# Low-rank products on the un-normed input, inverses in 16-token blocks joined by products, and a new order of the recurrence's front

## The chip, the cores and the metric

The kernel runs on one core of one Trainium2 chip. The metric is the device time of one execution in microseconds (us), as a median of runs. The engines named below are TensorE (PE in the profile; its weight loads are PEld), VectorE (DVE), ScalarE (ACT), GpSimd (POOL) and SyncE (SP, which here only issues transfers). Each engine takes its own instructions in order, and semaphores hold it until the data of another are there.

## The reference, cut to what matters

Two transformer blocks on 256 tokens with 1024 features, the first with 16 meta tokens ahead of them, so T = 272. The first block is: FFN, RWKV7 time mix, FFN, FFN, sparse attention, FFN. Everything is float32. The change lies in the time mix, which works on the normed input `h`:

```python
def rwkv7_time_mix(h, mix, w_r, w_k, w_v, w_o, w0, w1, w2, a0, a1, a2, g1, g2, k_k, k_a, r_k, ...):
    xx = jnp.pad(h, ((0, 0), (1, 0), (0, 0)))[:, :-1] - h          # the token before, minus this one
    xr, xw, xk, xv, xa, xg = h[None] + xx[None] * mix[:, None, None, :]
    r = xr @ w_r;  k = xk @ w_k;  v = xv @ w_v
    w_log = -softplus(-(w0 + jnp.tanh(xw @ w1) @ w2)) - 0.5         # w1: 1024 x 64
    a = sigmoid(a0 + (xa @ a1) @ a2)                                # a1: 1024 x 64
    g = sigmoid(xg @ g1) @ g2                                       # g1: 1024 x 160
    kk = k * k_k, normed per head of 64 (norm at least 1e-12)
    k = k * (1.0 + (a - 1.0) * k_a)
    decay = exp(-exp(w_log))
    # per head, state S of 64 x 64, for each token:
    #   S = S * decay + (S @ -kk) (kk * a)^T + v k^T ;  y = S @ r
    ...
    return ((yn + bonus) * g) @ w_o
```

## The kernel before, in words

Activations lie transposed, 128 features on the partitions, eight tiles (KT) of T = 272 tokens. A product of float32 numbers is three products of rounded halves: `mm3` (L260) multiplies hi by hi (L261), lo by hi (L262) and hi by lo (L263). Activations are split into such halves by ACT (`xh`) and VectorE (`xl`, L440), weights by ACT (`wh`, L173) and VectorE (`wl`, L182). Weights come in units of 128 x 1024, by transfers on SP's queue into a ring; `run` and `ahead` load and split some units ahead. A projection of one 128-wide output tile (k0 to k7, v0 to v7, r0 to r7) is one unit of 8 x 3 products of 272 columns.

The time mix (`rwkv`) does not scan token by token. It works in chunks of 64 tokens. Its front is:

- The sums of squares of the first FFN's output (`sumsq`, a hook of the out-projection) go through two products with a matrix of ones (L306, L307) to `rstd`. `first_mix` then makes per tile the normed input `hn` (L499), the difference `xx` (L501, in the buffer kbx) and the mixes: x2 for k (L489, split into xh and xl), x1 and x4 for the low-rank w1 and a1 (also L489, unsplit, xm). A generator `mg` makes x5 for g1 (L463, unsplit).
- `first` does the units k0 to k2 with the 32 low-rank records of w1 and a1 between them (L594, plain f32 products of 272 columns). `l1_unit` does the same for g1 later (L614). The second factors follow (`l2w`, `l2a`, L639).
- Per k unit, `ev_k` squares on ACT (L562) and copies to kf; `ev_kb` sums the squares over a head by a product (L569) and takes the floor (L570, VectorE) into `rn`.
- `decay_a` scans the log decays (L654), `decay_b` takes their exponentials (L663 into AR, L664 in place, `pinv`), `units` the inverse norms (L681, L682) and kk (L684), `keys`, `removal` and `over` multiply the scaled keys (L691 to L717). AR and KB are then the two operands of the products within a chunk, `aab` (L738, L741), evacuated into the tile `tf`/`Dg` (L743).
- `inverses` inverts the unit triangular blocks of 32 tokens, 128 of them side by side, on VectorE: `start` transposes (L874), `rows` eliminates row by row (L868 multiplies, L871 adds, in two halves; the last rows by L885), `end` transposes back (L891, L892). The 16 meta tokens have a small one, `meta` (tile am). Chunks join 32-blocks by doubling products (L1122, L1130).

What order all this has is written by hand in `ORDER`: `play` walks it, takes the names in `UNITS` as weight units and the others as calls between them. The Tile framework's scheduler then sets each engine's queue from that. `early` has slots (tag S), `rk` holds AR, kbx and the rest.

## Time and profile before

| what | us |
|---|---|
| median of 3 runs | 1543.95 (1542.97 to 1545.03) |
| profiled execution, its own time | 1543.19 |
| profiled execution, its span | 1541.3 |
| TensorE busy | 1478.7 (96%) |
| VectorE busy | 1001.5 (65%) |
| ACT busy | 742.6 (48%) |
| mean granted TensorE clock | 0.988 |

The profile is of one execution. Its times count from the start of its span. A busy share is an average over stages with different limits, so the stage is read on its own: which engine is busy in it throughout, and what the others wait for. The granted clock is that of TensorE, where 1.00 is 2.4 GHz and 0.5 is 1.2 GHz. The time mix's front is the stretch from 214.55 us, where the last product of the first FFN ends, to 372 us.

### The profile page before, as it was taken

The page shows a single profiled execution, that of the slowest core. Times are in us where ns is not written, and L with a number is a line of the kernel's source. Part 1 is how long each engine was busy: PE and PEld are TensorE (multiplying, and loading weights), DVE is VectorE, ACT ScalarE, POOL GpSimd, SP SyncE. Part 2 cuts the span into 40 slices and gives each one's busy share as a digit, 9 for nine tenths or more (in the row PEclk, how much of TensorE's full clock was granted, in tenths as well). Part 3 has the DMA queues.
Part 4 walks back from the last instruction along what each step waited for, and adds up shares of the span by engine and source line. Part 5 has one row for each costly group of instructions (what it writes and reads, how often), then busy time and mean ns, then how long its engine had stood idle before and what let it go on. Part 6 is the DMA issues. An engine that isn't in the chain of part 4 may idle for free.

```text
span 1541.3 us, 30953 instructions
## 1 busy us (share of the span) xinstructions
PE 1478.7 (96%) x12612; PEld 1391.7 (90%) x12612; DVE 1001.5 (65%) x1887; ACT 742.6 (48%) x1284; POOL 261.5 (17%) x298
## 2 busy tenths in 40 slices
PE   7999989697999999999999998999999999999999
...
GB/s 227 211 171 167 175 132 123 87 97 69 43 2 178 177 174 164 174 198 169 175 174 164 182 120 59 23 198 192 190 177 185 186 142 96 87 223 190 187 195 99
...
## 3 DMA queue, kind: packets, MB, share of 16 engines
...
HBM read 226.52 MB, written 2.10 MB: 148 GB/s over the span
## 4 chain that ended last, share of the span: by engine, by line
PE 81%; DVE 12%; ACT 3%; issue 2%; DMA 2%; POOL 1%; SPq 0%; DVEq 0%; POOLq 0%; ACTq 0%
PE mm L261 22%; PE mm L263 22%; PE mm L262 22%; DVE wl L182 2%; PE mm L1896 1%; PE mm L1170 1%; PE mm L1169 1%; DMA wf<-ffn_in 1%; PE mm L1171 1%; PE mm L1898 1%; PE mm L1873 1%; PE mm L994 1%; PE mm L1840 1%; PE mm L802 1%; ACT L L1852 1%
## 5 line engine op out<-in xcount | busy, mean ns | idle before, releaser
L173 ACT ACTIVATE wh<-wf 128x1024 fp32r<-128x1024 f32 (+2 forms) x410 | 418.0, 1021 | 543.2 <-issue 277.9
L182 DVE TENSOR_TENSOR wl<-wf,wh 128x1024 fp32r<-128x1024 f32 (+2 forms) x402 | 479.1, 1193 | 144.8 <-PE mm L263 99.6
L261 PE MATMUL mm<-xh,wh 128*128 128x272 f32 (+2 forms) x1888 | 542.4, 289 | 13.4 <-ACT wh L173 8.3
L263 PE MATMUL mm<-xh,wl 128*128 128x272 f32 (+2 forms) x1888 | 541.2, 288 | 3.3 <-DVE wl L182 3.3
L262 PE MATMUL mm<-xl,wh 128*128 128x272 f32 (+2 forms) x1888 | 541.5, 288 | 2.9 <-DVE xl L440 2.5
L261 PEld LDWEIGHTS mm<-xh,wh 128*128 128x128 f32 (+1 forms) x1888 | 356.0, 189 | 18.9 <-ACT wh L173 9.2
L262 PEld LDWEIGHTS mm<-xl,wh 128*128 128x128 f32 (+1 forms) x1888 | 356.2, 189 | 6.1 <-DVE xl L440 3.2
L263 PEld LDWEIGHTS mm<-xh,wl 128*128 128x128 f32 (+1 forms) x1888 | 356.6, 189 | 4.8 <-DVE wl L182 4.5
L261 PE MATMUL mm<-hh,wh 128*128 128x272 f32 (+1 forms) x704 | 201.9, 287 | 0.0
L263 PE MATMUL mm<-hh,wl 128*128 128x272 f32 (+1 forms) x704 | 201.8, 287 | 0.0
L262 PE MATMUL mm<-hl,wh 128*128 128x272 f32 (+1 forms) x704 | 201.8, 287 | 0.0
L352 POOL TENSOR_TENSOR s<-s,rstd 128x272 f32<-128x272 f32 (+1 forms) x88 | 74.2, 845 | 443.9 <-ACT s L351 443.9
L261 PEld LDWEIGHTS mm<-hh,wh 128*128 128x128 f32 x704 | 132.7, 188 | 0.0
L263 PEld LDWEIGHTS mm<-hh,wl 128*128 128x128 f32 x704 | 132.6, 188 | 0.0
L262 PEld LDWEIGHTS mm<-hl,wh 128*128 128x128 f32 x704 | 132.5, 188 | 0.0
L360 DVE TENSOR_TENSOR u<-mm,s 128x272 f32<-128x272 f32 (+1 forms) x88 | 38.4, 437 | 124.8 <-PE mm L263 107.9
L182 POOL TENSOR_TENSOR wl<-wf,wh 128x1024 fp32r<-128x1024 f32 (+3 forms) x44 | 85.4, 1944 | 114.4 <-PE mm L263 38.6
L298 POOL TENSOR_TENSOR acc<-acc,sq 128x272 f32<-128x272 f32 (+1 forms) x48 | 41.5, 864 | 255.4 <-ACT sq L296 247.0
L350 DVE TENSOR_TENSOR t<-mm,rstd 128x272 f32<-128x272 f32 (+1 forms) x88 | 38.2, 436 | 70.7 <-PE mm L263 70.6
L262 PE MATMUL mm<-hid,wh 128*128 128x256 f32 x256 | 72.1, 282 | 0.0
L261 PE MATMUL mm<-hid,wh 128*128 128x256 f32 x256 | 72.1, 282 | 0.0
L263 PE MATMUL mm<-hid,wl 128*128 128x256 f32 x256 | 72.1, 281 | 0.0
...
## 6 DMA issues: line engine op xcount, KB each, us to landing
...
```

The costliest lines, as they stand in the source:

```text
L173: self.A.activation(u.wh, u.wf[:u.p, :u.n], AF.Copy)
L182: (self.V if u.lo == "V" else self.G).tensor_tensor(u.wl, u.wf[:u.p, :u.n], u.wh.bitcast(F32), op=ALU.subtract)
L261: self.mm(out, wh, xh, start=start, stop=False)
L262: self.mm(out, wh, xl, start=False, stop=False)
L263: self.mm(out, wl, xh, start=False, stop=stop)
L298: self.G.tensor_tensor(self.acc[:, :n], self.acc[:, :n], self.sq[:, :n], op=ALU.add)
L350: V.tensor_tensor(t[:, :n], st.pop(("g", m))[:, :n], r, op=ALU.mult)
L352: G.tensor_tensor(s[:, :n], s[:, :n], r, op=ALU.mult)
L360: V.tensor_tensor(u[:, :n], st.pop(("u", m))[:, :n], st.pop(("s", m))[:, :n], op=ALU.mult)
L802: mm(p[:, :T], wf[:w, s], R["lo"][1 + z][:w], start=z == 0, stop=z == 1)
L994: mm(ps[h][:, j * w:(j + 1) * w], flat(src(c, m)[OWN[h]]), R["AR"][OWN[h], m, j0:j0 + n, tok(c)], start=True, stop=True)
L1169: self.mm(out, xh, wh, start=start, stop=False)
```

## The change

Four edits come together.

1. `first_factors`, between gate/up and the out-projection of the first FFN, loads the first low-rank factors and makes w·mix and w·(1 − mix) from them, split into halves. The out-projection's hook splits its output with the gain but without the norm. `low_rank` then does 5 sums of 8 x 3 products on that un-normed input. `ev_l1` multiplies the sums by rstd (each token's own for one factor, shifted by a token for the other) and adds them. L594, L614 and the mixes x1, x4 and x5 are gone.
2. The split mix of k lies in the room of AR (tag "AR"). The floor of the squares is a Relu with a bias on ACT.
3. `inverses` inverts blocks of 16 instead of 32 tokens, both blocks of a 32-block in one operation, 15 rows of two operations; `turned`, `joined` and `added` then join the two by 128, 128 and 64 small products.
4. A new `ORDER` of the front, up to r2; from there it is the old one.

```diff
@@ ORDER, its front
-ORDER = ("mg evk2 evk0 mg mg k3 evk1 l2w evkb2 k4 evkb1 evk3 mg evkb3 decay_a mv mv mv evkb0 l2a k5 k6 evk4 mg "
...
+ORDER = ("lwa k0 lg1 l2w k1 evk0 l2a evk1 evkb0 k2 lg2 tri evk2 evkb1 decay_a k3 mv evk3 evkb2 k4 mv mv evkb3 evk4 "
...
@@ swiglu
+        if between:
+            between()
         self.out_proj(wout, KFF, lambda: st["h"], 0.5, t0, n, hook)
@@ first_factors (new), per factor of 128 columns
+                for s, i in mixes:
+                    o = VEC["mix"] + 8 * i
+                    V.tensor_tensor(b[:, :, s], w[:, :, s], self.vec[:, o:o + KT, None].to_broadcast([128, KT, s.stop - s.start]),
+                                    op=ALU.mult)
+                V.tensor_tensor(a, w, b, op=ALU.subtract)
...
+                    for x in (a, b):
+                        t = slot("l1", F32R, 2 * KT * n)
+                        o = t.rearrange("p (j k c) -> p j k c", j=2, c=n)
+                        A.activation(o[:, 0], x, AF.Copy)
+                        V.tensor_tensor(o[:, 1], x, o[:, 0].bitcast(F32), op=ALU.subtract)
...
+        prepare(0, 128, ((slice(0, 64), 1), (slice(64, 128), 4)))
+        prepare(128, 128, ((slice(0, 128), 5),))
+        prepare(256, 32, ((slice(0, 32), 5),))
@@ first_mix
-            hi, lo = R["x", 2] = [self.xs.tile([128, KT, T], F32R, tag=n, name=n) for n in ("xh", "xl")]
...
+            x2 = R["pool"].tile([128, 2, KT, T], F32R, tag="AR", name="xk")
+            hi, lo = R["x", 2] = x2[:, 0], x2[:, 1]
...
-                for i in (1, 4):
-                    mix(R["x", i][:, k, :T], i, k)
@@ enter
             self.rms(T)
+            low_rank()
             first_mix()
@@ new
+        def low_rank():
+            ps = R["l"] = [self.psum() for _ in range(5)]
+            for k in range(KT):
+                for i, p in enumerate(ps):
+                    w, s = self.l1[i // 2], slice(128 * k, 128 * k + 128) if i < 4 else slice(64 * k, 64 * k + 128)
+                    w = w[i % 2] if i < 4 else w
+                    self.mm3(p[:, :T], w[0][:, s], w[1][:, s], self.xh[:, k, :T], self.xl[:, k, :T], k == 0, k == KT - 1)
+
+        def ev_l1(j):
...
+                V.tensor_tensor(f, p[:n, :T], self.rstd[:n], op=ALU.mult)
+                V.tensor_tensor(y[:, 1:], q[:, :T - 1], r[:, :T - 1], op=ALU.mult)
+                V.tensor_tensor(f[:, 1:], f[:, 1:], y[:, 1:], op=ALU.add)
+                if j == 0:
+                    A.activation(f[:64], f[:64], AF.Tanh)
+                else:
+                    A.activation(f, f, AF.Tanh, scale=0.5)
+                    V.tensor_scalar(f, f, 0.5, 0.5, op0=ALU.mult, op1=ALU.add)
@@ ev_kb
-                V.tensor_scalar(R["rn"][:, m], ss[:, :T], 1e-24, None, op0=ALU.max)
+                A.activation(R["rn"][:, m], ss[:, :T], AF.Relu, bias=self.eps[:, 4:5])
@@ decay_b
+            AR = R["AR"] = R["pool"].tile([128, NP, 2, T], F32, tag="AR", name="AR")
@@ inverses
         def rows(s0, s1):
...
             for s in range(s0, s1):
...
+                m, w = n - 1 - s, s + 1
+                u = self.tmp("u")[:, :2 * m * w].rearrange("p (b i j) -> p b i j", b=2, j=w)
+                below = both(t, w, 0, (B, m), (1, w))
+                V.tensor_tensor(u, both(a, s, w, (1, m), (0, w)), both(t, s, 0, (0, m), (1, w)), op=ALU.mult)
+                V.tensor_tensor(below, below, u, op=ALU.add)
+        def turned():
...
+            V.transpose(Dg[:, :n], tf[:, :, :n].rearrange("p s t -> p t s"))
+            V.transpose(Dt, tf)
+            p = R["p16"] = self.psum()
+            for c in range(32):
+                for r in quads:
+                    mm(p[r, c * n:c * n + n], Dg[r, :, c], Dg[r, :n, c], start=True, stop=True)
+        def joined():
+            V.transpose(Dg[:, n:], tf[:, :, n:].rearrange("p s t -> p t s"))
+            self.A.activation(tf[:, :, :n], byblk(R.pop("p16")), AF.Copy)
+            G.memset(tf[:, :, n:], 0.0)
+            p, o = R["p16"] = self.psum(), self.psum()
+            for c in range(32):
+                for r in quads:
+                    mm(p[r, c * n:c * n + n], tf[r, c], Dt[r, n:, c], start=True, stop=True)
+                for r in quads[::2]:
+                    mm(o[r, c * n:c * n + n], Dt[r, :, c], tf[r, c, :n], start=True, stop=True)
+        def added():
...
+            V.tensor_tensor(x, byblk(p), x, op=ALU.add)
+            for r in quads[::2]:
+                x = Dg[r, :n].rearrange("p t c -> p c t")
+                V.scalar_tensor_tensor(x, byblk(o)[r], self.eps[r, 2:3], x, op0=ALU.mult, op1=ALU.add)
-        cuts = (0, 5, 10, 15, 20, 25, 31)
-        return [start, meta] + [lambda a=a, b=b: rows(a, b) for a, b in zip(cuts[:-1], cuts[1:])] + [end]
+        cuts = (0, 5, 10, 15)
+        return [start, meta] + [lambda a=a, b=b: rows(a, b) for a, b in zip(cuts[:-1], cuts[1:])] + [turned, joined, added, end]
@@ the program
-        c.swiglu(*ffn(0, 0), *full, lambda k: c.sumsq(k, c.h[:, k]), [c.positions(first), c.bias_rows(first)])
+        c.swiglu(*ffn(0, 0), *full, split("norm", 8, *full), [c.positions(first), c.bias_rows(first)], c.first_factors)
```

Line numbers of the changed kernel are 2 higher than before's through most of the file's first part (L261 becomes L263). Three places of the order, engine by engine:

TensorE behind the last product of the first FFN, before: the two products for the norm (on acc and sq) stand next to each other, and the first k product and the low-rank ones (L594, xm by the weight in wf) follow.

```order
L263 MATMUL mm<-hh,wl 128x272
L306 MATMUL mm<-acc,mats 128x272
L307 MATMUL mm<-sq,mats 128x272
L261 MATMUL mm<-xh,wh 128x272
L594 MATMUL mm<-xm,wf 64x272
```

And after, at the same place, to the product on sq (L309); the low-rank weights are the tiles named l_:

```order
L265 MATMUL mm<-hh,wl 128x272
L308 MATMUL mm<-acc,mats 128x272
L263 MATMUL mm<-xh,l_1768 128x272
L264 MATMUL mm<-xl,l_1768 128x272
L265 MATMUL mm<-xh,l_1768 128x272
...
L263 MATMUL mm<-xh,l_1796 128x272
L264 MATMUL mm<-xl,l_1796 128x272
L265 MATMUL mm<-xh,l_1796 128x272
L263 MATMUL mm<-xh,l_1768 128x272
L309 MATMUL mm<-sq,mats 128x272
```

31 of the 120 low-rank products now stand between the product on acc and the one on sq.

ACT around the exponentials of the decay, before: the exponential into AR (L663) comes while k units are still to be squared and copied (L562, L239).

```order
L301 ACT_TABLE_LOAD
L681 ACTIVATE kbx<-kbx 128x1088
L663 ACTIVATE AR<-pinv 128x8x272
L173 ACTIVATE wh<-wf 128x1024
L466 ACTIVATE xmh<-t 128x272 x2
L682 ACTIVATE kbx<-kbx 128x1088
L173 ACTIVATE wh<-wf 128x1024
L562 ACTIVATE s<-mm,vec 128x272
L239 ACTIVATE kf<-mm 128x272
```

And after (L627 is the floor of the squares as a Relu, L665 the exponential into AR, L503 and L508 the mixes of r):

```order
L618 ACTIVATE s<-mm,vec 128x272
L241 ACTIVATE kf<-mm 128x272
L503 ACTIVATE s<-hn,vec 128x272 x2
L627 ACTIVATE kbx<-mm,eps 128x272
L503 ACTIVATE s<-hn,vec 128x272
L627 ACTIVATE kbx<-mm,eps 128x272
L303 ACT_TABLE_LOAD
L665 ACTIVATE AR<-pinv 128x8x272
L683 ACTIVATE kbx<-kbx,eps 128x1088
```

The exponential moved behind the last square, copy and floor of the k units.

TensorE between v7, r0 and r1, before: copies of the keys and values (L970, L982) and the meta products (L1008) follow r0.

```order
L263 MATMUL mm<-xh,wl 128x272
L970 MATMUL mm<-mats,kbx 16x128 x16
L982 MATMUL mm<-mats,vf 16x128 x8
L1008 MATMUL mm<-AR,kbx 16x16 x32
L261 MATMUL mm<-xh,wh 128x272
```

And after, the join's products of `joined` (L913, L915) follow the same copies, 32 pairs of rows like the two shown; those of `turned` (L903, 128 of them) stand ahead of r0:

```order
L265 MATMUL mm<-xh,wl 128x272
L1006 MATMUL mm<-mats,kbx 16x128 x16
L1018 MATMUL mm<-mats,vf 16x128 x8
L913 MATMUL mm<-af,tf 32x16 x4
L915 MATMUL mm<-tf,af 32x16 x2
```

L1008 (now L1044) moved behind r1, and the joins came in between.

## Rows read from the trace of the kernel before

**Rows 1.** The page, TensorE's busy tenths in 40 equal slices of the span.
```profile
PE   7999989697999999999999998999999999999999
```
**Rows 2.** Stretches: length, busy PE, PEld, DVE, ACT, POOL (count), clock, DMA, GB/s.
```profile
219.15:241.65 22.50, 18.79 (x91) 11.89 (x92) 22.50 (x57) 5.14 (x11) 3.25 (x5) 0.85 0.00 1
241.65:269.91 28.26, 27.43 (x173) 24.09 (x173) 22.00 (x37) 24.25 (x46) 0.37 (x2) 1.00 0.54 168
269.91:302.32 32.41, 20.76 (x368) 19.61 (x370) 30.32 (x66) 21.79 (x39) 1.20 (x2) 0.90 0.33 102
302.32:359.07 56.75, 47.13 (x624) 37.60 (x617) 55.30 (x210) 20.31 (x35) 9.16 (x15) 0.95 0.30 94
359.07:371.98 12.91, 11.36 (x171) 9.75 (x172) 4.14 (x11) 6.33 (x12) 4.18 (x4) 0.55 0.00 1
371.98:457.00 85.02, 82.02 (x1342) 67.53 (x1341) 53.77 (x123) 33.94 (x78) 10.10 (x12) 1.00 0.11 33
```
**Rows 3.** Waits of TensorE, 214.55 to 372 us: total us, times, longest.
```profile
PE mm L738 <- DVE AR L717: 8.8, 2, 7.9
PE mm L1122 <- DVE tf L891: 6.2, 1, 6.2
PE mm L261 <- ACT xh L504: 5.1, 1, 5.1
PE mm L741 <- issue: 3.1, 2, 2.1
...
PE mm L1130 <- ACT H L239: 1.5, 2, 1.1
```
**Rows 4.** A stretch of the first FFN, columns as above.
```profile
140.00:150.00 10.00, 10.00 (x82) 10.00 (x81) 5.92 (x9) 4.83 (x8) 1.86 (x2) 1.00 0.59 185
```
**Rows 5.** Timeline at the norm: start, length, engine, line, what, count, [idle before].
```profile
215.89 0.72 PE L307 MATMUL mm<-sq,mats 128*128 128x272 f32 x2 [0.88 <-ACT sq L296]
...
218.67 0.44 DVE L287 SCALAR_TENSOR_TENSOR rstd<-u,rstd 128x272 f32<-128x272 f32 x1
```
**Rows 6.** Groups of VectorE, 214.55 to 302.32 us: count, busy us, mean ns.
```profile
L489 DVE SCALAR_TENSOR_TENSOR xm<-kbx,vec,hn 128x272 f32<-128x272 f32 x16 | 7.2, 489 | 0.0
...
L570 DVE TENSOR_SCALAR kbx<-mm 128x272 f32<-128x272 f32 x8 | 3.2, 430 | 0.0
```
**Rows 7.** Timeline of ACT at the decay's exponential.
```profile
264.64 2.03 ACT L663 ACTIVATE AR<-pinv 128x2176 f32<-128x2176 f32 x1 [0.72 <-DVE pinv L654]
```
**Rows 8.** Timeline: first aab product, AR's end, inverse's transpose, first doubling product.
```profile
285.84 0.24 PE L738 MATMUL mm<-AR,kbx 64*32 64x32 f32 x5 [0.95 <-DVE AR L717]
...
300.99 1.40 DVE L717 TENSOR_TENSOR AR<-AR 128x252 f32<-128x252 f32 x4
...
310.69 2.08 DVE L874 STREAM_TRANSPOSE af<-tf 128x1024 f32<-128x1024 f32 x1
...
359.07 1.10 PE L1122 MATMUL mm<-tf,Tt 32*32 32x32 f32 x32 [6.21 <-DVE tf L891]
```
**Rows 9.** Groups of VectorE, 302.32 to 359.07 us.
```profile
L871 DVE TENSOR_TENSOR tf<-tf,u 128x110 f32<-128x110 f32 (+32 forms) x54 | 11.4, 243 | 0.1
L868 DVE TENSOR_TENSOR u<-af,tf 128x110 f32<-128x110 f32 (+32 forms) x54 | 11.4, 248 | 0.0
L182 DVE TENSOR_TENSOR wl<-wf,wh 128x1024 fp32r<-128x1024 f32 x8 | 9.7, 1209 | 0.0
L871 DVE TENSOR_TENSOR am<-am 128x15 f32<-128x15 f32 (+7 forms) x15 | 2.9, 194 | 0.1
...
L628 DVE TENSOR_SCALAR lora<-lora 128x272 f32<-128x272 f32 (+1 forms) x2 | 1.5, 771 | 0.0
```
**Rows 10.** Timeline of TensorE behind r0.
```profile
330.91 1.93 PE L970 MATMUL mm<-mats,kbx 128*16 128x128 f32 x32
...
334.52 0.69 PE L1008 MATMUL mm<-AR,kbx 64*16 64x16 f32 x64
```
**Rows 11.** The stretch of the first four aab.
```profile
285.84:290.04 4.20, 2.09 (x182) 1.98 (x184) 4.20 (x11) 1.96 (x4) 0.00 (x0) 1.00 0.45 141
```

188 lines of the change are left out of this document (78 added, 110 removed), and 10 rows, old and new, of the table ORDER.

## The prediction

> **What bounds the kernel now.** The page comes first. TensorE is busy nearly everywhere; its thin place is slices 6 to 10 of 40, some 193 to 385 us, with 6 and 7 tenths in the 8th and 10th [rows 1]. That is the front of the RWKV mixer, and every edit lies in it or just ahead of it. Split by stage [rows 2], the front reads: from the norm to 241.65 us VectorE is busy for all of 22.50 us; to the end of the k projections (269.91) TensorE is, for 27.43 of 28.26; then VectorE again, for 30.32 of 32.41 and 55.30 of 56.75, with TensorE idle for 11.7 and 9.6 us of the two and its clock at 0.90 and 0.95; then 12.91 us at a clock of 0.55; from 372 to 457 TensorE is the bound again. The waits say on what TensorE waits there: the decayed keys (L738 on AR, the longest 7.9 us), the inverse (L1122 on the transposed tf, 6.2 us), and the first mix after the norm (L261 on xh, 5.1 us) [rows 3]. So the front is a chain of VectorE work with TensorE filling it, and a saving counts where it moves the end of the last doubling product and the r products behind it (372 us in the trace). I replayed the new order with the durations of the trace, each engine taking its instructions in its own order; the results are below.
>
> The sum is made against the profiled run's own 1543.19 us. The median of the runs, 1543.95, lies 0.8 us above it. A change under 0.2% (3.1 us) can't be told from none in this kernel's measurement.
>
> **Weights made ahead (first_factors).** Some ten VectorE operations and six copies, about 11 and 5 us, stand between gate/up and the out-projection of the first FFN. There VectorE is busy for 5.92 of 10 us and TensorE for all of it, 82 products of 272 columns in 10 us, 0.122 us each [rows 4]. TensorE's cover hides them: 0, at most 2 us if a weight split comes late. The splits of the input in the out-projection's hook lie under its products as the squares did. They are 16 operations, and the last ones have the time that the final products leave.
>
> **The norm, 2.9 us later.** Before, the product with the squares starts at 215.89, and rstd is done 2.54 us after its end, at 219.15 [rows 5]. After, 31 low-rank products stand ahead of it on TensorE: 31 x 0.122 = 3.8 us from 214.9, so it starts at 218.8 and rstd is done at 218.8 + 0.72 + 2.54 = 222.05. In return TensorE isn't idle until 221.69; it does 120 products (14.6 us) up to 230.6, for most of which it had no other work.
>
> **The k projections, 6.3 us shorter.** VectorE sets the pace up to 241.65 and loses 16 xm mixes for the low-rank inputs (7.2 us), 8 of the same kind for the gate (3.6) and 8 floors of the squares (L570, 3.2), which ACT takes [rows 6]: 14.0 us. It gains nine operations of 272 columns at L570's 0.43 and two of the kind of L628 at 0.77 [rows 9], 5.4 us, where the norm is put on the sums. Net 8.6 us. TensorE loses the f32 products of L594 here and of L614 later. In the replay 6.3 of the 8.6 us arrive: TensorE now waits for the tanh of the decay (2.9 us), for free banks (1.3) and for one square (1.4), places where it didn't stand still before. The last k product ends at 222.05 + (269.91 - 219.15 - 6.3) = 266.5, 3.4 us earlier.
>
> **Decays and keys, where the gain is eaten.** The split mix of the k input now lies in the room of AR, so the decay's exponential can't start before the last k product. Before, it started at 264.64, 5.3 us ahead of that product's end, between the k units' own ACT work [rows 7]. After, ACT still has the squares and floors of the last k units and a table load to do, so it starts about 4 us after that end. From there ACT does two large exponentials and four half ones, and VectorE the products of L686, the keys and the removals, with the mixes of r and weight splits between; the replay has the first aab product 28.4 us after the last k product, at 294.9, and AR complete at 300.4. Before, the first came at 285.84, but the second half of them waited for AR, done 302.3 [rows 8]. So TensorE idles from 277 to 295 after v0 to v2, and then has aab, v3 and v4 together. af is transposed at 313, against 312.77 before: the 3.4 us are gone. The nearest short price is the one of before: 21.2 us from that exponential's start to the first aab; with it the first aab comes 3.2 us earlier.
>
> **The inverse, 30 us less on VectorE, and TensorE late in its place.** Before, from 312.77 to the first doubling product at 359.07 VectorE does 54 + 54 row operations, 22.8 us, between other work, the last rows by L885 and the first of two transposes [rows 8, 9]. After, 15 x 2 operations of about 0.25 (7.4 us; the rows of before with most columns are that long), the 30 of the meta block (0.19 each, 5.8), two weight splits (2.4) and a half transpose, half of L874's 2.08 (1.0): 16.6 us, done at 329.6 and, with what starts L903, 329.9. TensorE by then has idled since 320, v7 being done. It then has, in order: 128 small products (L903) 4.4, r0 24 x 0.122 and a little for its start, 3.0, the copies of L1006 and L1018 3.6 [rows 10], 192 joining products (L913, L915) 5.5, r1 to r4 12.0, and L1044, L1056, L1073 and L789, each between the 0.69 and 1.93 us of L1008 and L970 [rows 10], 4.5: 33.0 us, to 362.9. Nothing on VectorE is late any more; TensorE is. The first doubling product came at 359.07 before, so this point is 3.8 us later.
>
> The joins' price is the open one. 320 products are 640 records. The cheapest rows are L1008's, 64 records in 0.69 us: 6.9 us. The aab products at 285.84 to 290.04 take 4.20 us for 182 records with a 2.1 us "issue" pause among them [rows 3, 11], 23 ns each: 14.8 us. I take 9.9, nearer to L1008's, since both are 16 columns wide and no such pause stands behind L1008, and keep 6.9 to 14.8 for the range.
>
> A sentence apart on a page: the Trainium skill, "TensorEngine Tiling (Array Packing)", section Instruction Overhead, gives each matmul about 60 cycles however few its columns, and advises against cutting a side that is already small; at 2.4 GHz that is an estimate of 25 ns a record, 16 us for 640, and by it the sum would come out at +3.9 instead of -2.2. L1008's 10.8 ns a record [rows 10] speaks against it for products in row groups that can overlap, the pause among aab for it.
>
> **What comes back.** From 359.07 to 371.98 TensorE did its work at a clock of 0.55, the lower level, after 6.2 us of idling; 11.36 us busy [rows 2, 3]. After, it comes to the same work from 33 us without a pause, at the upper level: 11.36 x 0.55 = 6.2 us if the clock alone sets it, and 6.9 with half of the 1.5 us that the doubling's second product waits for H. So the r products end at 362.9 + 6.9 = 369.8, against 371.98. From there the order is that of before, and TensorE is busy for 82.02 of 85.02 us [rows 2]; nothing more is gained.
>
> **Sum:** +2.9 - 6.3 + 3.6 (af at 313 instead of 312.77, so the whole lead is gone) + 3.6 (TensorE's tail instead of the inverse) - 6.0 (the low clock and the rest of its waits) = -2.2 us. 1543.19 - 2.2 = **1541.0**.
>
> **Rivals.**
> *A, the forecast (0.45):* as summed, -6 to +2: 1538 to 1545; half of it is below the bound of 3.1 us from the median, half within.
> *B, faster, the chain behind the k units is as short as before (0.25):* the exponential to aab takes 21.2 us (-3.2) and the joins 6.9 (-3.0): -8.4, 1535, with 1531 to 1538. For it: VectorE has 8.6 us less to do between the norm and aab. Against: the replay finds the keys' half exponentials queued behind the mixes of r and the weight splits on ACT.
> *C, slower, the joins are paid per record (0.19):* at the low clock or with pauses like 2.10 us, 640 records cost 28 ns each, between 23 and L1122's 34 (32 records in 1.10 us at the clock of 0.55 [rows 2, 8]): 17.9 us instead of 9.9, +8.0 on TensorE's tail, which nothing covers. -2.2 + 8.0 = +5.8: 1549. It decides from 24 ns a record on (3.1 + 2.2 = 5.3 us above 9.9, over 640). For it: TensorE comes to L903 after ten idle us, as it came to L1122, and that stretch ran at 0.55.
> *D, nothing arrives (0.11):* the k phase is no shorter, since the tanh, bank and square waits (5.6 us) grow by the missing 3 and take all of it: 1544, within the bound.
>
> **How the numbers follow.** Faster: half of A and B, 0.22 + 0.25 = 0.47. Same: the other half and D, 0.23 + 0.11 = 0.34. Slower: C, 0.19. The range takes in A, B to its middle and C: 1532 to 1550.
>
> **What would show it.** Right: rstd near 222; the last k product near 266.5; L665 after it and no aab before 292; TensorE idle for over 10 us ahead of aab; inverse's rows done near 330 with TensorE waiting for them, L903 and the joins near 10 us together; a clock of 1.00 at the doubling products. Wrong: L665 with aab soon after (B), a pause or a clock near 0.5 in L903 to L915 (C), or a wait of an FFN product for a weight split in 140 to 160 us. The forecast's weakest step is the 28.4 us to aab: a queue of two engines, replayed by hand, that moves the end one for one.

## The result: slower by 1.3%, and where the time went

The changed kernel takes **1565.22 us**, median of 4 runs (1563.96 to 1565.28), against 1543.87 (1542.97 to 1545.03) for the kernel before on the same chip: a ratio of 1.0132, 95% interval 1.0119 to 1.0144, 21.3 us more. The forecast was 1541, and its range ended at 1550. The profiled execution has a span of 1562.9 us and a mean granted clock of 0.977 (before 1541.3 and 0.988).

TensorE's slices of the page answer to [rows 1]. The thin place has become thinner: 5, 6 and 8 tenths in the 8th to 10th slice instead of 6, 9 and 7.

```profile
PE   7999999568999999999999999999999999999999
PEclk9999998778999999999999999899999999999999
```

By stages (stretch, its length, busy us of PE, PEld, DVE, ACT and POOL with counts, granted clock, DMA share, GB/s), cut at the same events as [rows 2] where they exist: rstd, the end of the first L639 products, last k product, first aab product, first product of the inverse (L903), first doubling product, end of r5, and the 85 us behind it:

```profile
221.63:239.84 18.21, 15.63 (x95) 13.60 (x94) 16.18 (x42) 7.70 (x16) 2.76 (x3) 0.87 0.01 1
239.84:274.73 34.89, 34.89 (x213) 32.11 (x213) 21.12 (x34) 21.75 (x48) 1.91 (x3) 0.87 0.42 128
274.73:303.19 28.46, 10.26 (x76) 9.53 (x76) 21.80 (x40) 22.32 (x33) 0.37 (x2) 0.76 0.25 84
303.19:337.84 34.65, 22.08 (x537) 21.44 (x537) 32.69 (x115) 11.87 (x25) 7.62 (x15) 0.84 0.23 78
337.84:382.67 44.83, 39.49 (x956) 36.74 (x956) 18.09 (x29) 14.01 (x18) 5.88 (x6) 0.78 0.14 44
382.67:393.20 10.53, 10.14 (x175) 8.96 (x172) 4.97 (x13) 2.66 (x10) 0.00 (x0) 0.84 0.21 75
393.20:478.20 85.00, 82.00 (x1342) 67.51 (x1341) 53.85 (x123) 33.85 (x78) 10.13 (x12) 1.00 0.11 33
```

TensorE's waits in 214 to 372 us answer to [rows 3] (engine, line, releaser: total us, times, longest):

```profile
PE mm L740 <- DVE AR L719: 17.3, 1, 17.3
PE mm L903 <- DVE tf L898: 12.6, 1, 12.6
PE mm L639 <- ACT lora L598: 2.6, 1, 2.6
PE mm L1056 <- DVE room L1047: 1.5, 1, 1.5
PE mm L915 <- issue: 1.3, 1, 1.3
PE mm L913 <- issue: 1.3, 1, 1.3
PE mm L903 <- issue: 1.1, 1, 1.1
```

And the points in time that the sum was built on (start, length, engine, line, what; the third is TensorE's first aab product, the fourth its first product of the inverse, the last the first doubling product; [rows 5], [rows 7] and [rows 8] are their like of before):

```profile
221.19 0.44 DVE L289 SCALAR_TENSOR_TENSOR rstd<-u,rstd 128x272 f32<-128x272 f32 x1
279.66 2.03 ACT L665 ACTIVATE AR<-pinv 128x2176 f32<-128x2176 f32 x1
303.19 0.34 PE L740 MATMUL mm<-AR,kbx 64*32 64x32 f32 x8 [17.27 <-DVE AR L719]
337.84 0.47 PE L903 MATMUL mm<-tf 32*32 32x16 f32 x18 [12.57 <-DVE tf L898]
382.67 0.74 PE L1158 MATMUL mm<-tf,Tt 32*32 32x32 f32 x20
```

Behind r5 nothing differs: 82.00 us busy of 85.00, before 82.02 of 85.02 [rows 2]. So the whole loss lies between the norm and r5. From the start of the norm's first product (L306, now L308) to the end of r5 it is 157.75 us before and 179.05 after, 21.3 more. **This stage** is the measure for the experiments, since a single execution's total moves by some us with the FFN ahead of it (the norm starts at 213.5 to 219.8 us in the runs below). Against the forecast the stage is 23.4 us longer, and the places are plain from the events:

| from, to | forecast | measured | off by |
|---|---|---|---|
| start to rstd | 222.05 | 221.63 | -0.4 |
| rstd to last k product | 44.45 | 53.10 | +8.65 |
| last k product to first aab | 28.4 | 28.46 | +0.1 |
| first aab to L903 | 35.0 | 34.65 | -0.35 |
| L903 to first doubling product | 33.0 | 44.83 | +11.8 |
| first doubling product to r5's end | 6.9 | 10.53 | +3.6 |

**The k phase.** TensorE waits 2.6 us for the tanh of the decay's factor (L639 on lora), and falls to the lower clock 0.4 us behind its end. From 239.84 us to the last k product it is busy for 34.89 of 34.89 us, but for much of that at half the pace. Windows of TensorE after (columns as above):

```profile
230.00:235.00 5.00, 2.42 (x18) 2.16 (x17) 5.00 (x14) 2.90 (x5) 2.11 (x2) 1.00 0.00 0
235.00:240.00 5.00, 5.00 (x13) 3.23 (x11) 3.08 (x8) 3.12 (x8) 0.65 (x2) 0.50 0.02 3
240.00:245.00 5.00, 5.00 (x16) 3.81 (x17) 1.45 (x3) 1.41 (x3) 0.75 (x2) 0.50 0.11 13
245.00:250.00 5.00, 5.00 (x26) 4.81 (x26) 5.00 (x9) 2.37 (x5) 1.16 (x2) 0.64 0.23 92
```

At 0.50, 0.50 and 0.64 these 15 us hold 5 + 5 + 3.6 us at the lower level, which is some 7 us of lost work; with the wait, 9.4. (The expectation of k3_tiles below names another wait of 2.2 us, for the mix; the trace has none there: 15.63 us busy of 18.21 leaves room for the 2.6 alone.)

**TensorE's tail.** L903 and the joins, with r0 between them, in windows (L903; r0; the copies L1006 and L1018; L913 and L915; r1; the rest up to the first doubling product):

```profile
337.84:343.00 5.16, 4.08 (x257) 3.93 (x257) 0.98 (x1) 0.00 (x0) 0.00 (x0) 0.50 0.01 3
343.00:348.20 5.20, 5.20 (x24) 5.05 (x24) 1.08 (x1) 0.60 (x1) 0.52 (x1) 0.56 0.01 3
348.20:351.80 3.60, 3.60 (x49) 3.11 (x48) 2.67 (x4) 3.40 (x5) 0.00 (x0) 1.00 0.09 18
351.80:361.30 9.50, 6.98 (x386) 6.73 (x385) 0.00 (x0) 0.59 (x1) 0.00 (x0) 0.64 0.16 53
361.30:366.10 4.80, 4.80 (x42) 4.65 (x44) 3.30 (x4) 3.58 (x4) 3.43 (x4) 0.65 0.01 3
366.10:382.67 16.57, 14.83 (x220) 13.27 (x215) 10.06 (x20) 5.84 (x8) 1.93 (x2) 1.00 0.25 82
```

Each run of small products is followed by a wide projection at the lower level: r0 takes 5.2 us where 3.0 were counted, r1 4.8. The clock fell to 0.64 in the joins although TensorE came to them from 8.8 us of unbroken work, the last 3.6 at 1.00.

### The profile page after: what moved, and what is told of

Its sections match the earlier page's. It is cut to its first block, busy times and chain, and to the rows that moved or that the text cites. A ratio compares the mean times of both kernels' runs of the same rounds, so it can differ in the third digit from the quotient of the medians.

```text
span 1562.9 us, 32251 instructions
## 1 busy us (share of the span) xinstructions
PE 1492.2 (95%) x13292; PEld 1418.6 (91%) x13292; DVE 997.2 (64%) x1803; ACT 752.7 (48%) x1304; POOL 263.6 (17%) x300
## 4 chain that ended last, share of the span: by engine, by line
PE 85%; DVE 8%; ACT 3%; DMA 2%; issue 2%; POOL 0%; SPq 0%; DVEq 0%; ACTq 0%
PE mm L263 23%; PE mm L265 23%; PE mm L264 23%; PE mm L1932 1%; DMA wf<-ffn_in 1%; DVE wl L184 1%; PE mm L1206 1%; PE mm L1205 1%; PE mm L1207 1%; PE mm L1909 1%; PE mm L1934 1%; PE mm L1030 1%; PE mm L639 1%; PE mm L1876 1%; PE mm L804 1%
## 5 line engine op out<-in xcount | busy, mean ns | idle before, releaser
L263 PE MATMUL mm<-xh,wh 128*128 128x272 f32 (+1 forms) x1824 | 527.1, 289 | 9.7 <-ACT wh L175 9.7
L265 PE MATMUL mm<-xh,wl 128*128 128x272 f32 (+1 forms) x1824 | 524.9, 288 | 2.4 <-DVE wl L184 2.4
L264 PE MATMUL mm<-xl,wh 128*128 128x272 f32 (+1 forms) x1824 | 523.5, 287 | 0.0
L263 PEld LDWEIGHTS mm<-xh,wh 128*128 128x128 f32 x1824 | 346.2, 190 | 12.4 <-ACT wh L175 10.5
L265 PEld LDWEIGHTS mm<-xh,wl 128*128 128x128 f32 x1824 | 345.9, 190 | 3.7 <-DVE wl L184 3.3
L264 PEld LDWEIGHTS mm<-xl,wh 128*128 128x128 f32 x1824 | 345.5, 190 | 0.5 <-DVE xl L320 0.2
L263 PE MATMUL mm<-hh,wh 128*128 128x272 f32 (+1 forms) x704 | 201.7, 287 | 0.0
L263 PEld LDWEIGHTS mm<-hh,wh 128*128 128x128 f32 x704 | 132.6, 188 | 0.0
L263 PE MATMUL mm<-hid,wh 128*128 128x256 f32 x256 | 72.0, 281 | 0.0
```

The lines of the kernel that those rows point to most:

```text
L263: self.mm(out, wh, xh, start=start, stop=False)
L264: self.mm(out, wh, xl, start=False, stop=False)
L265: self.mm(out, wl, xh, start=False, stop=stop)
```

## The experiments

Seventeen runs. Where no interval is given it is one execution with its profile, beside the kernel before on the same chip; such a time moves by some 6 us with the FFN ahead of the norm, so the verdicts go by the stage. A stage has a spread of its own: old_inv, dup, warm, spread, r0_first and v_early change nothing ahead of the last k product, and yet that point comes 57.3 to 60.5 us after the norm's start (the changed kernel: 60.6), since behind the wait for the tanh the lower clock lasted 6.8 us in one and up to 13.7 in another. So the table gives this part by itself, and up to 3.2 us of a stage is not its edit's doing. All are edits of the changed kernel unless it says otherwise.

| run | us (before, same chip) | stage, us | of it to the last k product |
|---|---|---|---|
| kernel before | 1543.87 | 157.75 | 55.5 |
| changed kernel | 1565.22 (1543.87) | 179.05 | 60.6 |
| k3_tiles | 1562.06 (1548.45) | 172.2 | 52.6 |
| old_inv | 1555.77 (1548.45) | 165.95 | 59.0 |
| k3_old | 1551.78 (1548.24) | 161.5 | 53.9 |
| inv_late | 1555.10 (1548.45) | 168.0 | 55.5 |
| dup | 1578.29 (1545.60) | 188.3 | 58.9 |
| warm | 1564.56 (1548.24) | 179.3 | 60.5 |
| spread | 1557.69 (1548.24) | 168.9 | 57.3 |
| spread_k3 | 1555.07 (1545.60) | 168.8 | 52.6 |
| r0_first | 1563.60 (1547.38) | 172.9 | 59.0 |
| ar_early | 1576.83 (1548.24) | 187.3 | 69.3 |
| v_early | 1564.55 (1548.45) | 177.7 | 58.9 |
| best1 | 1562.73 (1547.38) | 170.8 | 52.6 |
| best2 | 1556.44 (1547.38) | 170.75 | 52.6 |
| best_old | 1545.99 (1547.38) | 156.6 | 52.6 |
| best_old_timed | 1542.89 (1544.48) | 156.8 | 52.6 |
| best_pool | 1553.96 (1545.60) | 164.6 | 52.6 |
| before_pool | 1552.33 (1545.60) | 165.3 | 55.5 |

### Undoing one part, then both: k3_tiles, old_inv, k3_old

**k3_tiles.** Before, k0, k1 and k2 took each tile of the k mix together, nine products a tile; after, k0 alone follows the mix, three a tile. This run takes the three together again and puts the decay's L639 behind them:

```diff
-ORDER = ("lwa k0 lg1 l2w k1 evk0 l2a evk1 evkb0 k2 lg2 tri evk2 evkb1 decay_a k3 mv evk3 evkb2 k4 mv mv evkb3 evk4 "
+ORDER = ("lwa lg1 k0 k1 k2 l2w evk0 l2a evk1 evkb0 lg2 tri evk2 evkb1 decay_a k3 mv evk3 evkb2 k4 "
...
+            for k in range(KT):
+                for j in range(3):
+                    s = slice(128 * k, 128 * k + 128)
+                    self.mm3(R["k", j][:, :T], held_k[j][0][:, s], held_k[j][1][:, s], R["x", 2][0][:, k], R["x", 2][1][:, k],
+                             k == 0, k == KT - 1)
```

Expected:

> The changed kernel with one edit: the units k0, k1 and k2 take each tile of the mix together, nine products a tile, as the kernel before did, and the second low-rank factor (L639) stands behind them. In the changed kernel k0 alone follows the mix, three products a tile; TensorE waits 2.6 us for the tanh and 2.2 us for the mix, and runs at a clock of 0.50 from 235 to 245 us. Theory 1 (the k phase is long since TensorE starves behind VectorE's mix and then runs at the low clock): the last k product comes 8 to 11 us earlier than 274.7, near 265, all behind it moves along, and the time is 1554 to 1557. Rival (the whole loss is the inverse's small products, and the wait of 17.3 us for AR swallows what is gained ahead of it): under 3 us gained, 1562 or more.

Measured: the stage is 6.9 us shorter, between the theory and its rival; the time, 1562.06 us, falls into the rival's range. The last k product ends 52.6 us after the norm's start instead of 60.6 (57.3 to 60.6 in the runs with the same k phase), and the wait for lora is gone. The windows that answer to those above (the norm is 4 us later in this execution):

```profile
231.00:236.00 5.00, 5.00 (x42) 5.00 (x41) 4.86 (x14) 1.06 (x3) 0.00 (x0) 1.00 0.01 2
236.00:241.00 5.00, 5.00 (x34) 4.36 (x32) 4.24 (x12) 3.62 (x7) 2.76 (x3) 1.00 0.02 3
241.00:246.00 5.00, 5.00 (x28) 3.79 (x28) 1.71 (x4) 2.47 (x7) 0.00 (x0) 1.00 0.00 0
```

1.00 throughout. So the k phase's loss goes with the wait behind k0 and the lower clock behind it; the first aab still comes 28.5 us after the last k product and TensorE's wait there is 17.3 us as before.

**old_inv.** The inverse of 32-token blocks of the kernel before in the changed kernel:

```diff
-                V.tensor_tensor(u, both(a, s, w, (1, m), (0, w)), both(t, s, 0, (0, m), (1, w)), op=ALU.mult)
-                V.tensor_tensor(below, below, u, op=ALU.add)
...
-        def turned():
-        def joined():
-        def added():
+                    row(V, a, t, u, s + 1, s, (s + 1, (s + B + 1) // 2, B))
```

Expected:

> The changed kernel with the inverse of before (32 rows on VectorE, no joins by products). Theory 1 (the joins cost TensorE more than the shorter inverse gives back: from L903 at 337.8 to the first doubling product at 382.7 it takes 44.8 us): the inverse starts at 322 as now and takes the 46 us of before, so the first doubling product comes near 369 instead of 382.7, then a stretch at the low clock as in the kernel before: r5 ends near 382 instead of 393, the time is 1553 to 1556. Rival (the joins are sound and the loss lies ahead of them): VectorE's 30 us come back on top, 1572 to 1580.

Measured: 13.1 us shorter, 11.5 of them behind the last k product, though TensorE now waits 8.8 us for tf ahead of the doubling products. Those 8.8 us are what the new inverse was to remove; its 320 products cost more than that.

**k3_old.** Both undone (the two diffs above):

> The changed kernel with both suspects undone: k0 to k2 take each tile of the mix together, and the inverse is that of before. Measured from the start of the norm's first product (L306 or L308) to the end of r5, since the runs differ by some us ahead of it: 157.8 us in the kernel before, 179.1 in the changed one, 165.9 with the old inverse alone and 172.2 with the three k units alone. Theory 1 (the two losses lie one behind the other on one chain and add): 157 to 160, as the kernel before. Rival (a long wait for AR lies between them and swallows one): 162 to 166.

Measured: 161.5, between the two forecasts. The last k product comes 1.6 us earlier than before (53.9 against 55.5 us from the norm's start), the forecast's direction; but the first doubling product comes 147.9 us after it against 144.7, with 10.4 us of waiting for tf. So of the 21.3 us some 17.5 are the two undone parts, and 3.8 stay. The first aab product comes 11 us later than before, 82.4 us from the norm's start instead of 71.4, as the exponential waits for the last k product; that this is all of the 3.8 is argued from the trace, and best_old below, where the mixes of r no longer stand among the exponentials on ACT, has them back.

### The new inverse alone in the kernel before: inv_late

The inverse in 16-token blocks in the kernel before, with `turned` behind r1 and `joined` behind r2, so that TensorE always has wide work ahead of the small products:

```diff
-solve5 evv1 g1b solve6 solve7 evv5 solve8 v7 evv6 r0 evv7 ck0 evr0 dropv cv0 cm0 r1 evrb0 co0 r2 evr2 evr1
+evv1 g1b evv5 v7 evv6 r0 evv7 ck0 evr0 dropv cv0 cm0 r1 solve5 evrb0 co0 r2 solve6 solve7 solve8 evr2 evr1
```

> The kernel before with the new inverse alone (blocks of 16, joins by products), and with the first products (turned) behind r1 and the joins behind r2 in the order, so that TensorE reaches them without a wait and at the full clock. Theory 1: TensorE has 320 more small products, 10 to 14 us with the pauses of 1.1 to 1.3 us seen in the changed kernel, and loses the wait of 6.2 us for the inverse and most of the 5 to 6 us of low clock behind it: 0 to 3 us slower than before, 1543 to 1547. Rival (the inverse on VectorE is what limits, a shorter one is worth its time wherever it stands): 5 to 9 us faster, 1535 to 1539.

Measured: the stage is 10.2 us longer than before's, and both numbers missed. L906 here (the products of `turned`) takes 7.6 us and the joins 10.4, 18.1 for 640 records, near rival C's 17.9, though in part by pauses longer than C's. Here wide work stands ahead of the small products without a wait, and the clock falls all the same. Windows of the wide products, of the small ones to 338.20, and of the small ones from 338.30 to the next pause:

```profile
325.00:335.18 10.18, 10.18 (x160) 9.35 (x158) 6.91 (x13) 6.91 (x12) 0.24 (x1) 1.00 0.38 107
335.18:338.20 3.02, 2.76 (x180) 2.66 (x182) 1.23 (x1) 1.04 (x1) 0.00 (x0) 1.00 0.27 46
338.30:339.04 0.74, 0.74 (x52) 0.63 (x44) 0.00 (x0) 0.00 (x0) 0.00 (x0) 0.50 0.70 288
```

Ahead of the fall TensorE did 10 us of wide work without a pause and 3 us of small products with one pause of 0.26 us. Two of the pauses, in the timeline (in brackets the idle time ahead and what ended it):

```profile
337.00 2.04 PE L906 MATMUL mm<-tf 32*32 32x16 f32 x128 [0.26 <-issue]
342.10 0.69 PE L906 MATMUL mm<-tf 32*32 32x16 f32 x33 [3.06 <-issue]
```

128 records in 2.04 us and then 3.06 us in which TensorE waits for no engine that the trace shows.

### The price of a small product: dup

The joins' 384 records issued twice over; the second time they write the same results again, so it is added work alone:

```diff
-            for c in range(32):
+            for c in [x % 32 for x in range(64)]:
```

> The changed kernel with the 384 records of the joining products issued twice over (the second time they write the same results again), so 384 more small records behind the first and nothing else. Theory (each small record costs 25 ns at either level of the clock, and supply pauses come on top): these records cost what the first 384 did, 9.5 us with their pauses, so the stage from the norm to r5 is 9 to 11 us longer, 188 to 190, with two or three more issue pauses of over 1 us. Rival (the 9.5 us of the first pass were mostly its late start and the low clock it came in with): the second pass takes 4 to 6 us and has no pause; stage 183 to 185.

Measured: 188.3, 9.3 us longer, in the theory's range. The k phase came out 1.7 us shorter here; behind it the loss is 10.9 us. The records themselves take 18.3 us in the trace where the changed kernel's take 9.5, so 8.8 us for 384 more; the rest falls in the work behind them. The trace splits the price. Windows of the first 271 records, the other 497, and the wide r1 behind them, three of the pauses in the second, and what the instruction queue moved from 354.00 to 372.42 us (packets, MB, share):

```profile
354.10:358.50 4.40, 4.31 (x272) 4.11 (x271) 0.00 (x0) 0.59 (x1) 0.00 (x0) 1.00 0.29 104
358.50:372.40 13.90, 9.69 (x498) 9.33 (x498) 0.00 (x0) 0.00 (x0) 0.00 (x0) 0.55 0.02 5
372.40:377.70 5.30, 5.30 (x36) 5.15 (x37) 3.31 (x3) 4.08 (x4) 3.92 (x4) 0.57 0.01 3
```
```profile
359.84 0.20 PE L913 MATMUL mm<-af,tf 32*32 32x16 f32 x1 [1.39 <-issue]
363.29 0.24 PE L913 MATMUL mm<-af,tf 32*32 32x16 f32 x3 [0.92 <-issue]
366.75 0.23 PE L915 MATMUL mm<-tf,af 32*32 32x16 f32 x1 [0.98 <-issue]
```
```profile
q8 instruction: 6, 0.10, 2.1%
```

The first 271 take 16 ns each at 1.00 with no pause. Behind them there is a pause of about 1 us every 125 to 128 records, and the records between take 19.5 ns at 0.55 (9.69 us for 498): 28 ns each all told. The clock fell to the lower level in the middle of the small products and stayed there in r1. The profile names the pauses only "issue"; its DMA packets say what they are. Six packets of 16384 bytes on the instruction queue go with these 768 records, 128 a packet and one every 3.4 to 3.5 us, and each pause ends 1.38 to 1.48 us after a packet has been moved. So it is in all runs: the 38 "issue" pauses of over 0.8 us between 200 and 400 us of the traces end 1.2 to 1.6 us after such a packet. In inv_late's two longest (3.06 and 2.9 us) the packet began only 0.7 and 0.5 us after the pause had. The 2.1 us among the aab products of before [rows 3] is one of them. So these are waits for instructions, as far as packets and pauses can show it. 128 records take 2.0 us (inv_late) to 2.5 us (dup), a packet comes every 3.4, and that, 27 ns a record, is the price of a long run here. What sets the 1.2 to 1.6 us is not shown.

### Is it the idling before, or the small products themselves: warm, spread, spread_k3, r0_first

**warm.** 136 and 100 wide products whose result nobody reads, placed in TensorE's waits ahead of aab and of L903:

```diff
+            "warm0": warm(136), "warm1": warm(100),
...
+                for i in range(n):
+                    mm(p[:, :T], R["x", 3][0][:, i % KT, :128], R["x", 3][1][:, i % KT], start=True, stop=True)
```

> The changed kernel with 136 products that nobody reads in TensorE's wait ahead of the first aab (17.3 us) and 100 ahead of L903 (12.6 us): the work and the waits stay, only TensorE is not idle in them. Theory 1 (idling costs TensorE its clock, and the small products and r0 behind it run at 0.50): aab at 1.00 instead of 0.50, but the inverse then waits for VectorE, so little there; L903, r0 and what follows lose 4 to 7 us: 1558 to 1561. Rival (the small products are slow whatever the clock, by their own length and by the supply of instructions): under 1.5 us, 1563 to 1566.

Measured: 179.3, no gain. The stretch ahead of the small products, L903's stretch, r0's and the joins':

```profile
325.00:337.00 12.00, 11.42 (x90) 11.20 (x88) 11.90 (x48) 2.76 (x6) 2.38 (x5) 1.00 0.43 132
337.00:343.00 6.00, 4.32 (x257) 4.25 (x258) 1.77 (x3) 0.18 (x1) 0.01 (x1) 0.74 0.01 3
343.00:348.00 5.00, 5.00 (x30) 4.84 (x31) 1.06 (x2) 0.71 (x2) 0.52 (x1) 0.63 0.01 3
351.00:361.00 10.00, 6.98 (x389) 6.53 (x386) 0.20 (x1) 0.82 (x2) 0.00 (x0) 0.80 0.15 54
```

TensorE enters L903 at 1.00, with a wait of 1.2 us left right ahead of it, and leaves it at the lower level all the same. So the theory that it was the ten idle us (rival C's "for it" said so too) falls: here as in inv_late, which has no such wait, the clock comes down among the small products themselves.

**spread.** `joined` hands out its 32 groups of products, and r1 and r2 take 12 products' records behind every three wide ones. (`turned` hands out its own to r0 likewise, but in the trace r0 runs ahead of them, and they stand in a row of 192 and one of 64.)

```diff
+                    for k in range(KT):
+                        s, x = slice(k * 128, k * 128 + 128), R["x", i]
+                        self.mm3(p[:, :T], wh[:, s], wl[:, s], x[0][:, k, :T], x[1][:, k, :T], k == 0, k == KT - 1)
+                        for _ in range(n):
+                            R["spread"].pop(0)()
...
-            for c in range(32):
+            def join(c):
```

> The changed kernel with the 192 joining products (L913, L915) not in one piece but 12 at a time behind every three products of r1 and r2. Theory 1 (the pauses of 1.1 to 1.3 us named issue, one after some 128 small records, are TensorE waiting for its instructions, and vanish among longer products; r1 runs at the full clock): 2 to 5 us less, 1560 to 1563. Rival (the joins cost their 9.5 us wherever they stand): within 1 us of the changed kernel, 1564 to 1566.

Measured: 168.9, 10.2 us shorter; both numbers missed. Two windows in r1 and r2 with the joins in them:

```profile
346.30:355.00 8.70, 8.70 (x265) 7.27 (x267) 0.74 (x2) 1.41 (x2) 0.00 (x0) 1.00 0.01 2
355.00:366.00 11.00, 10.61 (x293) 8.58 (x286) 4.56 (x11) 0.78 (x2) 0.00 (x0) 1.00 0.18 51
```

The clock stays at 1.00 and no pause comes. But the joins got no cheaper: r1 with its 192 records takes 8.3 us (346.33 to 354.62) where its wide products alone were counted at 3.0, so 27 ns a record, 10.5 us for the 384 against 9.5 in a row. From the first small product to the first doubling product it is 38.0 us, 44.8 in the changed kernel and 40.3 in r0_first below, which has r0 in the same place. So 4.5 us of the gain come from r0, which in this order fell into the wait for the inverse, 2.3 from the spreading, with r1 at the full level, and 3.2 are a shorter k phase, in which the clock came back sooner.

**spread_k3.** spread and k3_tiles together:

> The joins spread between the products of r1 and r2, together with k0 to k2 interleaved tile by tile. Theory (two separate losses, 6.9 and 10.2 us when each was undone alone, part of the second being an earlier k phase by chance, 3.2): they add up to 13 to 14 us, stage 165 to 167, time 10 to 14 us below the changed kernel, still above the kernel before. Rival (spread's gain was the clock level with which it came to the joins, and that is chance): the small records run at the low level, r1 and r2 with them, stage 169 to 173.

Measured: 168.8, the rival's range, but not for its reason: the joins ran at 1.00 (9.00 us busy of 9.00). The first aab came 4.7 us earlier than in spread, and then r0 waited 6.1 us for its mix (ACT, L508; in spread 6.7) and L933, this kernel's L903, 3.7 us for VectorE. The gain of the k phase ended in the next VectorE wait.

**r0_first.** r0 ahead of the inverse's products instead of behind them:

```diff
-evv7 dropv solve5 r0 ck0 evr0 cv0 solve6
+evv7 dropv r0 solve5 ck0 evr0 cv0 solve6
```

> The changed kernel with r0 ahead of L903 in the order instead of behind it. The run with the spread joins came out 10.2 us shorter from the norm's first product to the end of r5 (168.9 against 179.1), but its order also brought r0 into TensorE's wait ahead of L903. Theory (that is where most of it came from, and the joins cost the same in one piece or in twelve): r0's 5.4 us at the low clock go into the wait, 172 to 175 us from the norm to r5, about 1559 to 1561. Rival (the spreading did it): 177 to 179, 1563 to 1566.

Measured: 172.9, in the theory's range for the stage: r0 in the wait instead of at the lower level behind L903. 4.5 of the 6.1 us lie behind the k phase, the rest ahead of it. The time, 1563.60, is above the theory's.

### The late exponential: ar_early, v_early

**ar_early.** The k mix in the room of the un-normed input instead of AR's, and the exponentials right behind k7:

```diff
-            x2 = R["pool"].tile([128, 2, KT, T], F32R, tag="AR", name="xk")
-            hi, lo = R["x", 2] = x2[:, 0], x2[:, 1]
+            hi, lo = R["x", 2] = [self.xs.tile([128, KT, T], F32R, tag=n, name=n) for n in ("xh", "xl")]
```

> The changed kernel with the split mix of k in the room of the un-normed input (as the mixes of r later) instead of AR's, and the decay's exponentials in the order behind k7 instead of behind all k units' copies. Theory 1 as predicted (AR's room makes the exponential late, and the wait for the first aab is the price): the exponential starts some 8 us ahead of the last k product's end, the first aab 6 to 10 us earlier than 303, and the time falls by 5 to 9: 1556 to 1560. Rival (VectorE and ACT have so much to do there that an early exponential only changes their order): 0 to 3 us, 1562 to 1565.

Measured: 187.3; both numbers missed. The first aab now comes 25.3 us after the last k product, 3.1 sooner, but not by rival B's price: from the exponential to the first aab it is 26.5 us, where B had 21.2. And the mix must wait for the end of the low-rank products, and the last k product comes 69.3 us after the norm's start instead of 60.6. A room of its own for the mix was not tried.

**v_early.** v3 to v5 ahead of aab, in the 17.3 us wait:

> The changed kernel with v3, v4 and v5 ahead of the first aab instead of among and behind them: TensorE idles there for 17.3 us. Theory 1 (order: the idle spell ahead of aab is filled and aab is done sooner): three units of 3.2 us go into the idle spell, the aab come together, the inverse starts 4 to 7 us earlier than 322 less up to 3.7 us for three weight splits that VectorE does sooner; 1559 to 1563. Rival (VectorE sets the time to aab, and each split ahead of them moves them one for one): aab 3.7 us later, no gain, 1564 to 1566.

Measured: 177.7, 1.4 shorter, and the k phase alone, which the edit doesn't touch, is 1.7 shorter: no gain, the rival's number. The work moved out of the way only made the wait for the inverse longer, 15.4 us instead of 12.6.

### Is there a version that beats both: best1, best2, best_old, best_pool, before_pool

**best1** takes k3_tiles, v0 to v6 ahead of aab, r0 to r2 ahead of L903 and the joins spread over r3 and r4; **best2** moves the mixes of r on ACT behind the keys as well:

```diff
+                        with tc.issue_after(R["keyed"].ins):
                             A.activation(p, R["hn"][:, k, :T], AF.Copy, scale=self.v("mix", 8 * i + k))
```

> The changed kernel rearranged by what the runs showed: k0 to k2 take each tile together, v0 to v6 stand ahead of the first aab, r0 to r2 ahead of L903, the joins lie among r3 and r4. The work is that of the changed kernel. Theory (its loss is order: TensorE idles 17.3 and 12.6 us ahead of its own backlog): 7 us from the k units, 3 to 4 from aab in one piece, 5 from r0, and r1 and r2 for the joins to hide behind: 155 to 160 us from the norm to the end of r5 (157.8 in the kernel before), so the time is within 3 us of the kernel before. Rival (the small products and the late exponential cost what they cost): 163 to 168, 6 to 10 us slower than the kernel before.

> As the run before in this call, and ACT takes the mixes of r only behind the keys (L691 before), so that the exponentials and the keys come first in its queue. Theory (ACT's queue between the last k product and the first aab, 28.5 us in all of these runs, holds some 3 to 5 us of mixes that can wait): the first aab comes 3 to 5 us earlier after the last k product, and the time falls by as much, or by less where r0 then waits for its mix. Rival (VectorE sets it): within 1 us of the run before.

Measured: 170.8 and 170.75; both theories missed, and best2 came out at its rival's number. In best1 the joins were not spread as the program asks: the schedule put 21 of r3's 24 wide products ahead, then 168 of the joins' records in a row, and only the rest in groups between wide products. Windows of the three:

```profile
350.71:355.95 5.24, 5.24 (x24) 4.91 (x22) 0.93 (x2) 0.03 (x1) 0.53 (x1) 0.51 0.01 3
355.95:358.60 2.65, 2.65 (x170) 2.62 (x169) 0.00 (x0) 0.00 (x0) 0.00 (x0) 1.00 0.03 6
358.60:371.90 13.30, 13.30 (x249) 10.85 (x250) 2.49 (x5) 1.75 (x2) 0.00 (x0) 0.52 0.13 42
```

The clock had come back to 1.00 behind the wide products and fell again behind the 168 small ones, and the groups were done at the lower level, though TensorE was busy for 13.30 of 13.30 us; in spread the groups began at 1.00 and kept that. best2 has the same run of 168 records and the same groups at 0.50 behind it. There the first aab came 78.2 us after the norm's start instead of 85.1, so the mixes of r had indeed stood in the way of the half exponentials, but then TensorE waited 8.3 us for VectorE ahead of r0's head sums (L820).

**best_old** has the old inverse, k3_tiles, v3 to v5 ahead of aab, r0 to r2 under the inverse and the mixes of r behind the keys. One execution, and then twelve:

> The same rearrangement with the inverse of before instead of blocks of 16 (v0 to v5 ahead of aab, k0 to k2 together, the mixes of r behind the keys, r0 to r4 during the inverse). Theory (with the inverse of before, VectorE's 46 us set the first doubling product, whatever TensorE has): it moves with the first aab, 146 to 150 us after the norm's first product (144.7 in the kernel before), and the time is 0 to 5 us over the kernel before. If it beats the run with the new inverse by 5 us or more, the joins aren't worth their products even when TensorE has its backlog done.

> The same kernel as best_old (the changed kernel with the old inverse, k0 to k2 interleaved tile by tile, v3 to v5 ahead of aab, r0 to r2 under the inverse and the mixes of r behind the keys), now timed in five rounds. Theory (its stage was 156.6 us against 157.75): 1 to 2 us faster than the kernel before, a ratio of 0.999. Rival (one look of the stage is within what the first FFN varies from run to run): a ratio of 1.000 to 1.003 with an interval that holds 1.

Measured: a stage of 156.6 and 156.8; 1542.89 us against 1544.48, a ratio of 0.9992, interval 0.998 to 1.0005. Against best2, which differs from it in the inverse, the place of v6 and what stands around the inverse, the stage is 14.1 us shorter, far over the 5 us that the expectation named. So with the new inverse taken out and the order mended, the low-rank products on the un-normed input and that order together are worth about 1 us of the stage and nothing that the time can show.

**best_pool** and **before_pool** move the weight splits of v4 to v7 and r0 to r4 from VectorE to GpSimd, in best_old and in the kernel before, since VectorE's queue is what the doubling waits for in both:

```diff
-"lov": "VVVVVVVV", "lor": "VVVVVVVV"
+"lov": "VVVVGGGG", "lor": "GGGGGVVV"
```

> The version with the old inverse, k0 to k2 interleaved, the mixes of r behind the keys on ScalarE, and nine of the weight splits of v and r moved from VectorE to GpSimd. Theory (VectorE's queue sets the doubling, which waited 5.7 us for the inverse; the splits take some 8 us of it away from under the inverse): stage 149 to 153 instead of 156.6, time 1540 to 1544 where the kernel before is 1547. Rival (GpSimd's splits are slower and TensorE waits for them, or GpSimd and VectorE get in each other's way): stage 156 to 162, with waits of TensorE for wl of GpSimd.

> The kernel before, with the same nine weight splits of v and r moved from VectorE to GpSimd and nothing else. Theory: 2 to 6 us faster than before, since its doubling waits 6.2 us for the inverse that shares VectorE with those splits (stage 152 to 156 instead of 157.75). Rival: GpSimd's splits come late and TensorE waits for wl; 0 to 6 us slower.

Measured: ratios of 1.006 (1.0034 to 1.0085) and 1.005 (1.0031 to 1.007), slower by 8 and 7 us: the rivals' numbers, but with no wait of TensorE for a GpSimd split in either list of waits. VectorE itself got slower. Its rows in before_pool, 310 to 360 us, answer to [rows 9]:

```profile
L871 DVE TENSOR_TENSOR tf<-tf,u 128x110 f32<-128x110 f32 (+32 forms) x54 | 15.4, 320 | 0.1
L868 DVE TENSOR_TENSOR u<-af,tf 128x110 f32<-128x110 f32 (+32 forms) x54 | 15.4, 323 | 0.0
```

320 ns a row instead of 243. In before_pool the 38 of these 108 operations that overlap one of the nine splits take 476 ns on the mean, the other 70 take 238. best_pool's timeline has a plain case, one operation of VectorE and one of GpSimd:

```profile
325.52 2.40 DVE L888 TENSOR_TENSOR am<-am 128x63 f32<-128x63 f32 x1
325.40 2.44 POOL L184 TENSOR_TENSOR wl<-wf,wh 128x1024 fp32r<-128x1024 f32 x1
```

An operation whose fellows take 0.2 us stands for 2.40, as long as the split beside it. A rule of the Trainium skill, "SBUF — State Buffer", section Who interferes with whom, is that a VectorE instruction with two inputs in SBUF contends with a GpSimd instruction that reads SBUF; the trace agrees.

## Why the prediction was wrong, step by step

- **Weights made ahead (0 to 2):** right. In 140 to 160 us TensorE is busy for 20.00 of 20 us, with VectorE at 19.45.
- **The norm (+2.9):** right, rstd at 221.63 instead of 222.05, +2.5.
- **The k projections (-6.3):** wrong, +2.3 measured. The replay had waits (5.6 us for tanh, banks and square; 2.6 came in this phase), but every product at its duration at the upper level. Behind the wait for the tanh the clock was at 0.50, and 13.6 us of the work were done at half the pace. The rows of before had shown the like: 0.85 in the stretch with the 5.1 us wait [rows 2, 3]. The step that failed is that durations were replayed and the clock was not; k3_tiles shows it, with no wait for lora, 1.00, and 8.0 us of it back. A second error was hidden by luck: in k3_tiles, which has the same products, TensorE is busy for 44.52 of the 45.08 us from rstd to the last k product, so the forecast's 44.45 us, with 5.6 us of waits in them, held some 5.7 us of its work too little. How the replay came to lose it is not on record.
- **Decays and keys (28.4 us from the last k product to aab):** right to 0.1 us, and named as the weakest step. It was not: the replay of the two queues held.
- **The inverse's rows (35.0 us from the first aab to L903):** right, 34.65.
- **TensorE's tail (33.0 us):** 44.83. L903 +0.8, r0 +2.2, the joins +4.0, and from there to the doubling +4.9 (r1 1.8 at the lower level, 1.5 of waiting for VectorE's room ahead of L1056, 0.7 for the first half of L1084, which the list left out, and 0.9 besides). The joins' price was the term called open: 640 records took 5.16 + 9.50 = 14.7 us, where the sum had 9.9 and the range ended at 14.8. So the bound held, and the choice of L1008's row, a burst of 64 records, was the mistake: a burst shorter than a packet of instructions (128 records in dup) can't stand for one of 256 or 384.
- **What comes back (-6.0):** -2.4. "It comes to the same work from 33 us without a pause, at the upper level" is refuted: four of those stretches were at 0.50, 0.56, 0.64 and 0.65, and of the 10.5 us behind the first doubling product the last 5 were at 0.66.
- **The rivals.** C was the right kind and side, by its mechanism (pauses and the lower level), but gave 1549: it charged the clock to the small records alone, not to the wide products behind them, r0, r1 and the r products of the doubling. Its reason, the idle time ahead of L903, is what warm and inv_late refuted. Of the k phase only D had that it might be no shorter, by longer waits; the waits came out shorter, and the clock made it longer.
- **The Trainium skill's price.** By the Trainium skill, "TensorEngine Tiling (Array Packing)", section Instruction Overhead, the prediction's estimate was 25 ns a record and 16 us for the 640 records. Measured were 14.7 us, nearer to that than to the 9.9 of the sum, and nearest to the 14.8 of the aab row. The trace shows it made up otherwise: 16 ns a record at 1.00 or 19.5 at 0.55, and the rest in pauses of about 1 us.

The whole, by differences to before: +2.5 (norm) + 2.3 (k phase) + 18.8 (last k product to first doubling: 107.9 us against 89.2) - 2.4 = +21.2 us, against 21.3 measured.

Two things stay open: what sets the 1.2 to 1.6 us between a packet of instructions and the next record, and why groups of small products among wide ones keep the level at which they begin. 1.00 in spread and spread_k3, 0.50 in best1 and best2 is what four runs show, and that is no rule.
